# A mixture-of-experts loop on one core: two paired If/Else ladders per expert become three exclusive regions in a row, with a hint for the jump over the long one

## Chip, cores and metric

One core of a Trainium2 chip runs the whole program. The metric is device time in microseconds (us) per execution, the median of several runs. The engines are called as the profile calls them: PE (TensorE matmul), PEld (TensorE weight load; TensorE's own sequencer instructions stand under PEldq), DVE (VectorE), ACT (ScalarE), POOL (GpSimd), SP (SyncE, which here issues the weights' DMAs). A letter q behind an engine's name means its sequencer: branches, register loads, semaphores.

## What is computed

Two layers of a backbone over 1024 latent and 256 context tokens of width 1024. Each layer has a mixer (attention, pooling, convolution) and then a hierarchical mixture of 32 experts: the best of 4 groups, and in it the best 2 of 8 experts, so each token goes to 2 experts. The change is in the second part alone:

```python
def hier_moe(h, w_rg, b_rg, w_re, b_re, wg, wu, wd):
    lg = (h @ w_rg).astype(jnp.float32) + b_rg
    gsel = jnp.argmax(lg, axis=-1)
    ...
    top_v, top_i = lax.top_k(le_sel, TOP_K_IN_GROUP)
    ...
```

For every expert the tokens routed to it are multiplied by its gate and up matrices (1024 x 512 each), silu(gate) * up goes through its down matrix (512 x 1024), and the result is weighted and added up per token. One expert's three matrices are 6.29 MB in fp32. How many tokens an expert gets is known only at run time.

## The kernel before

**Tokens and paths.** Tokens of an expert are taken in chunks of 128. A register `n` per expert holds the number of started half chunks of 64 tokens (`load_n`, L2229). With `n` = 1 (37 of the 64 experts in the two layers with these inputs) the expert runs `half` (L2085): 32 matmuls in plain fp32 that put up to 64 tokens through gate and up. With `n` = 2 (17 experts) it runs `full` (L2109): 48 matmuls on split fp32r operands, three to a product, where ACT makes the high part and DVE the low part of every weight slice (`ws`, `self.split`, L167 and L168). With `n` above 2 (10 experts) there is a second chunk and more, with further Ifs inside (L2268, L2272, L2303, L2309).

**The loop over the experts** (L2256) is unrolled 32 times per layer, and the code of all paths of all experts lies in one long program. Per expert: the register load of a later `n`, a gather of the tokens of expert e+2 on POOL, then **the first ladder** (L2264: `n` below 2, else L2267: `n` above 2, else `full`), whose arms are gate and up alone; then for all arms alike `act` (Silu on ACT and a product on DVE, L2138), the transposes of the next expert's tokens (`xt_pe`, L2053) and of the hidden values (`ht`, L2144), then **the second ladder** (L2298, L2301) around `down` (L2154), then `prep` of the next expert if that has `n` above 1 (L2321: five splits each on ACT and DVE, `prep`, L2080), `evac` (L2162) and two scatters on POOL (`scatter`, L2168). Every engine takes every branch for itself: it loads `n` into its own register and runs its own copy of the Ifs.

**Weights** come through a ring of 14 buffers of 1 MB, six per expert (four for gate and up, two for down). `e_loads` (L2012) lets SP issue the loads for as many units as its limit says, each behind the release of the buffer; it is called once behind the first ladder and once at the expert's end. `over` (L2247) gathers an expert's second chunk, under an If.

Of the kernel before, what the change touches and what calls it, by code (L numbers as in the profile page):

```python
# [30 lines left out]
ALPHA = (2 * DEPTH) ** 0.25  # L31
EPS = 1e-6
OOB = 1 << 24

NU, NU0 = 14, 10

# [105 lines left out]
class Kernel:  # L142
# [1885 lines left out]
    def moe(self):  # L2028
        tc, nc, l = self.tc, self.nc, self.l
        nt = self.nt  # L2030
        T = nt * 128
        with ExitStack() as ctx:
# [3 lines left out]
            xg = [sp.tile([128, D], F32, name=f"xg{i}") for i in range(5)]  # L2036
# [11 lines left out]
            def gather(buf, idx):  # L2048
                nc.gpsimd.indirect_dma_start(out=buf, out_offset=None, in_=self.h_d[0:T, :],
                                             in_offset=bass.IndirectOffsetOnAxis(ap=idx, axis=0),  # L2050
                                             bounds_check=T - 1, oob_is_err=False)
# [11 lines left out]
            def xt_copy(tps, n):  # L2063
                nc.scalar.activation(XT[n % 2][:, 0:4, :], tps[0], AF.Copy)
                nc.vector.tensor_copy(XT[n % 2][:, 4:8, :], tps[1])
# [12 lines left out]
            def prep(e):  # L2078

                for k in range(AHEAD):  # L2080
                    ws(e, k)
                    if k < 2:
                        xs(e, 0, k)

            def half(ps, e):  # L2085


                x = XT[e % 2]
                for k in range(KD):
                    w = self.unit(e, k // 2)[:, k % 2]  # L2090
                    for o in range(2):
                        nc.tensor.matmul(ps[0][64 * o:64 * o + 64, :], x[:, k, 0:64], w[:, :, o * 256:(o + 1) * 256],  # L2092
                                         start=(k == 0), stop=(k == KD - 1))
# [15 lines left out]
            def full(ps, e, x=None):  # L2109

                for k in range(KD - 2):
                    if k + AHEAD < KD:
                        ws(e, k + AHEAD)
                    prod(ps, 0, k)
                for o in range(2):
                    for k in range(KD - 2, KD):
                        prod(ps, 0, k, NS, (o,))
                    if x is not None and o == 0:
                        xt(x, e)

            def double(ps, p2, e, m):

                prod(ps, 0, 0)
                xt(xg[2 + e % 3], e)
                for k in range(1, AHEAD):
                    prod(ps, 0, k)
                if m > 4:
                    gather(xg[2 + e % 3], self.idx_g[:, 2, e:e + 1])
                xs(e, 1, 0)
                xs(e, 1, 1)  # L2130
                for k in range(KD):
                    prod(p2, 1, k, NS - 1)
                    if k + NS - 1 < KD:
                        ws(e, k + NS - 1, NS - 1)
                    if AHEAD <= k + NS - 2 < KD:
                        prod(ps, 0, k + NS - 2, NS - 1)

            def act(ps, o):  # L2138
                sg = SG[o]
                nc.scalar.activation(sg, ps[o][:, 0:256], AF.Silu)  # L2140
                nc.vector.tensor_tensor(sg, ps[o][:, 256:512], sg, op=OP.mult)  # L2141
                return sg
# [7 lines left out]
            def hidden(ps, g):  # L2150
                for o, s in enumerate((act(ps, 0), act(ps, 1))):
                    ht(ps, s, g, o)

            def down(g, e, hf, os=range(2)):  # L2154
                for k, o in [(k, o) for k in range(4) for o in os] if hf else [(k, o) for o in os for k in range(4)]:
                        c = slice(o * 512, o * 512 + 512)
                        z = k // 2 * 64
                        nc.tensor.matmul(py[o][64 * o:64 * o + 64, :] if hf else py[o],  # L2158
                                         g[:, k % 2, z:z + 64] if hf else g[:, k, :],
                                         self.unit(e, 4 + k // 2)[:, k % 2, c], start=(k == 0), stop=(k == 3))  # L2160

            def evac(y):  # L2162
                nc.scalar.activation(y[:, 0:512], py[0], AF.Copy)
                nc.vector.tensor_copy(y[:, 512:1024], py[1])  # L2164
# [16 lines left out]
            def places(e, j):  # L2181
                return [x[:, j, e:e + 1] for x in (self.idx_v, self.idx_w)]
# [58 lines left out]
                nc.gpsimd.memset(x, 0.0)  # L2241
            xt(xg[0], 0)
            self.e_loads(NU, nc.scalar)
            with tc.If(N[0] > 1):
                prep(0)

            def over(e):  # L2247
                with tc.If(N[e] > 2):
                    gather(xg[2 + e % 3], self.idx_g[:, 1, e:e + 1])
            load_n(1)  # L2250
            load_n(2)
            over(0)
            over(1)
            over(2)
            self.route_rows(sp)
            for e in range(NE):  # L2256
                n = N.pop(e)
                nxt = e + 1 if e + 1 < NE else None
                if e + 3 < NE:
                    load_n(e + 3)  # L2260
                if e + 2 < NE:
                    gather(xg[e % 2], self.idx_g[:, 0, e + 2:e + 3])
                ps, p2, y, y2, g, g2 = GU[e % 2], GU[1 - e % 2], Y[e % 2], Y[1 - e % 2], G[e % 2], G[1 - e % 2]
                with tc.If(n < 2) as c:  # L2264
                    half(ps, e)
                with c.Else():
                    with tc.If(n > 2) as c2:  # L2267
                        with tc.If(n < 4) as c3:  # L2268
                            full(ps, e, xg[2 + e % 3])
                            half(p2, e)  # L2270
                        with c3.Else():
                            with tc.If(n > 4) as c4:  # L2272
                                double(ps, p2, e, 5)
                                hidden(p2, g2)
                                down(g2, e, False)
                                evac(y2)
                                scatter(y2, places(e, 1))
                                more(e, n, 2, p2, g2)
                            with c4.Else():
                                double(ps, p2, e, 4)  # L2280
                    with c2.Else():
                        full(ps, e)
                self.e_loads(e * 6 + 4 + NU)
                pl = sp.tile([128, 2], I32, name="pl", bufs=4)
                for o, z in enumerate(places(e, 0)):
                    nc.vector.tensor_copy(pl[:, o:o + 1], z)
                if e + 3 < NE:
                    over(e + 3)
                s0, s1 = act(ps, 0), act(ps, 1)
                if nxt:  # L2290
                    x = xt_pe(xg[nxt % 2], (0,))
                ht(ps, s0, g, 0)
                if nxt:
                    x += xt_pe(xg[nxt % 2], (1,))
                ht(ps, s1, g, 1)
                if nxt:
                    xt_copy(x, nxt)
                with tc.If(n < 2) as c:  # L2298
                    down(g, e, True)
                with c.Else():  # L2300
                    with tc.If(n > 2) as c2:  # L2301
                        down(g, e, False, (0,))
                        with tc.If(n < 5) as c3:  # L2303
                            s0, s1 = act(p2, 0), act(p2, 1)
                            ht(p2, s0, g2, 0)
                            ht(p2, s1, g2, 1)
                            down(g, e, False, (1,))
                            evac(y2)
                            with tc.If(n < 4) as c4:  # L2309
                                down(g2, e, True)  # L2310
                            with c4.Else():
                                down(g2, e, False)
                            scatter(y2, places(e, 0))
                            for o, z in enumerate(places(e, 1)):
                                nc.vector.tensor_copy(pl[:, o:o + 1], z)
                        with c3.Else():
                            down(g, e, False, (1,))
                    with c2.Else():
                        down(g, e, False)
                if nxt:  # L2320
                    with tc.If(N[nxt] > 1):  # L2321
                        prep(nxt)
                evac(y)
                self.e_loads(e * 6 + 6 + NU)
                scatter(y, [pl[:, o:o + 1] for o in range(2)])
                if e >= NE - 3:
                    self.marks.append(nc.gpsimd.memset(self.spacer, 0.0))
                if e == 2:
                    self.route_gates()
# [147 lines left out]
```

## Time and profile before

| what | value |
|---|---|
| median of 3 runs | 3215.24 us (3214.84 to 3216.71) |
| the profiled execution | 3213.33 us, its span 3211.5 us, granted TensorE clock 0.918 |
| PE busy | 2635.0 us, 82% of the span |
| DVE, ACT, POOL busy | 1493.3, 1188.0, 1070.6 us |
| expert stage of the first layer | from about 845 us to 1650 us |
| expert stage of the second layer | from about 2374 us to 3148 us |

The span runs from the first to the last instruction; the profiled time is 1.8 us more. TensorE is the busiest engine, but its share is an average over stages of different kinds; what concerns the change is how TensorE's idle time is spread over the two expert stages.

### The profile page before, as it was taken

The numbers are of one execution on the slowest core, as the hardware profiler recorded it, in microseconds if no ns is written. First come the engines' busy times: TensorE is split into PE (matmuls) and PEld (weight loads), VectorE is DVE, ScalarE is ACT, GpSimd is POOL, SyncE is SP. The second block draws the span as 40 slices with busy tenths as digits, with TensorE's granted clock in tenths as the row PEclk, the third lists the DMA queues.
The fourth block names the chain that finished last, engine by engine and source line by source line (L and its number), as shares of the span: only waits on it lengthen the run. The fifth ranks groups of instructions, "written<-read, shape, count | busy, mean of one in ns | idle before, by whom it ended". The sixth has DMA issues, their size and how long they took to land. (4 is left out here: it accounts for less than half of the span.)

```text
span 3211.5 us, 41598 instructions
## 1 busy us (share of the span) xinstructions
PE 2635.0 (82%) x13118; PEld 1663.1 (52%) x13118; DVE 1493.3 (46%) x2851; ACT 1188.0 (37%) x2260; POOL 1070.6 (33%) x919
## 2 busy tenths in 40 slices
PE   6988899998488769879757989999957788798783
PEld 4766565576254435455227766666732344554331
DVE  3355556487543323334149555556851332333215
ACT  3223666632143323333135337665211322333212
POOL 1023999223311121211136349941331111111114
PEclk8998999999799889999878999999978899899997
DMA  7542000042778685757976530002279876645995
GB/s 270 215 142 74 1 1 1 1 158 85 277 297 335 231 310 184 278 188 264 360 295 193 183 136 1 1 1 96 88 260 380 312 288 248 233 158 203 340 361 230
DMA packets 280605, 616.63 MB, mean 192 GB/s; under 512 B 63376, under 2 KB 77072, under 8 KB 271504
## 3 DMA queue, kind: packets, MB, share of 16 engines
q1 hardware_dynamic: 251696, 562.24, 47.9%
q0 software_dynamic: 24544, 37.91, 3.4%
q10 hardware_dynamic: 3712, 8.88, 0.7%
q8 instruction: 275, 4.51, 0.6%
q14 instruction: 378, 3.10, 0.3%
HBM read 577.09 MB, written 73.81 MB: 203 GB/s over the span
## 5 line engine op out<-in xcount | busy, mean ns | idle before, releaser
L1327 DVE TENSOR_REDUCE mx<-S 128x1 f32<-128x1024 f32 (+1 forms) x272 | 215.3, 798 | 208.9 <-PE S L1322 208.5
L172 PE MATMUL gu<-wh,xh 128*128 128x512 f32 x432 | 188.8, 437 | 119.2 <-issue 100.5
L2158 PE MATMUL mpy<-er,g 128*128 128x512 f32 (+1 forms) x672 | 242.8, 630 | 9.9 <-issue 7.3
L2172 POOL DMA_INDIRECT y_d<-my,pl x128 | 140.8, 1100 | 321.5 <-ACTq L2264 108.8
L1339 ACT ACTIVATE P<-S,nb 128x256 f32<-128x256 f32 (+1 forms) x272 | 208.6, 773 | 33.7 <-DVE nb L1331 32.6
L1353 ACT ACTIVATE PT<-pt 128x512 f32<-128x512 f32 (+1 forms) x321 | 169.3, 532 | 135.5 <-PE pt L1344 126.9
L2141 DVE TENSOR_TENSOR sg<-gu,sg 128x256 f32<-128x256 f32 x152 | 57.6, 420 | 342.5 <-ACT sg L2140 337.5
L2171 POOL MEMSET spacer<- 128x1 f32 x152 | 17.6, 116 | 595.7 <-DMA y_d<-my,pl 330.0
L1344 PE MATMUL pt<-ident,P 128*128 128x128 f32 x1312 | 206.7, 282 | 10.1 <-ACT P L1339 10.0
L1388 PE MATMUL po<-PT,V 128*64 128x256 f32 x1312 | 212.5, 403 | 0.1
L2059 PE MATMUL mtp<-ident,xg 128*128 128x128 f32 x600 | 101.1, 300 | 133.7 <-issue 83.3
L178 POOL TENSOR_TENSOR rs_out<-ln_ve,mhalf 128x1 f32<-128x1 f32 x64 | 58.8, 919 | 444.4 <-DVE ln_ve L197 287.8
L2140 ACT ACTIVATE sg<-gu 128x256 f32<-128x256 f32 x152 | 50.3, 383 | 411.3 <-PE gu L2092 285.3
L173 PE MATMUL gu<-wl,xh 128*128 128x512 f32 x432 | 183.0, 424 | 9.0 <-DVE wl L168 9.0
L1344 PEld LDWEIGHTS pt<-ident,P 128*128 128x128 f32 x1312 | 145.3, 141 | 83.4 <-ACT P L1339 41.5
L174 PE MATMUL gu<-wh,xl 128*128 128x512 f32 x432 | 181.4, 420 | 4.3 <-issue 4.3
L168 DVE TENSOR_TENSOR wl<-er,wh 128x1024 fp32r<-128x1024 f32 x102 | 124.3, 1223 | 108.7 <-ACT wh L167 105.1
L172 PEld LDWEIGHTS gu<-wh,xh 128*128 128x128 f32 x432 | 88.9, 206 | 164.9 <-issue 140.2
L2164 DVE COPY my<-mpy 128x512 f32<-128x512 f32 x75 | 51.7, 690 | 260.0 <-PE mpy L2158 252.1
L1321 PE MATMUL S<-KH,Q 128*128 128x512 f32 (+1 forms) x400 | 168.8, 423 | 1.5 <-ACT P L1339 1.5
L2059 PEld LDWEIGHTS mtp<-ident,xg 128*128 128x128 f32 x600 | 77.8, 155 | 173.8 <-issue 125.2
L2092 PE MATMUL gu<-er,xT 128*64 128x512 f32 x720 | 161.4, 594 | 3.2 <-DVEq L2264 2.3
(381 smaller groups left out, 6410.1 us busy)
## 6 DMA issues: line engine op xcount, KB each, us to landing
er<-in_w_e_down SPq DMA_DIRECT2D x66, 1024.0 KB
er<-in_w_e_gate SPq DMA_DIRECT2D x130, 512.0 KB
er<-in_w_e_up SPq DMA_DIRECT2D x130, 512.0 KB
raw<-in_w_mod SPq DMA_DIRECT2D x40, 1024.0 KB
es<-in_w_e_gate SPq DMA_DIRECT2D x64, 512.0 KB
es<-in_w_e_up SPq DMA_DIRECT2D x64, 512.0 KB
es<-in_w_e_down SPq DMA_DIRECT2D x32, 1024.0 KB
raw<-in_w_e_gate SPq DMA_DIRECT2D x40, 512.0 KB
```

Of the source, the lines that this page charges most:

```text
L172: t.matmul(ps, lh, rh, start=start, stop=False)
L173: t.matmul(ps, lh, rl, start=False, stop=False)
L174: t.matmul(ps, ll, rh, start=False, stop=stop)
L1321: tens.matmul(x[:, c:c + w], q, self.KH[:, g, o:o + w], start=True, stop=False)
L1327: v.tensor_reduce(S[st, "mx"][:, ci:ci + 1], S[st, ci][:, 0:cs[ci][1]], axis=AX.X, op=OP.max)
L1339: act.activation(P[st][:, c:c + w], S[st, ci][:, :w], AF.Exp, bias=S[st, "nb"], accum_out=SU[pi][:, i, h, ci:ci + 1])
L1344: tens.transpose(tp[:, j, :], P[st][:, (g_ * 4 + j) * 128:(g_ * 4 + j + 1) * 128], self.ident)
L1353: act.activation(d, TP[st, g_][:, :m, :], AF.Copy)
L1388: tens.matmul(PO[key][o * 64:o * 64 + 64, :], self.V[:, k0(pi) + j, hp // 2, :], PT[pi, 2 * hp + o][:, j, :], start=(j == 0), stop=(j == n ...
L2059: nc.tensor.transpose(tp[:, j, :], x[:, k * 128:(k + 1) * 128], self.ident)
L2092: nc.tensor.matmul(ps[0][64 * o:64 * o + 64, :], x[:, k, 0:64], w[:, :, o * 256:(o + 1) * 256], start=(k == 0), stop=(k == KD - 1))
L2158: nc.tensor.matmul(py[o][64 * o:64 * o + 64, :] if hf else py[o], g[:, k % 2, z:z + 64] if hf else g[:, k, :], self.unit(e, 4 + k // 2)[:, ...
```

## The change

Per expert, the two ladders become three regions in a row that exclude each other: `n` above 2 first (label, and marked so that its body follows its branch directly), then `n` below 2, then `n` equal to 2. Each holds the expert's whole work (gate and up, activation, transposes, down). `small` does one activation and one `ht` where the common code did two. `prep` of the next expert and the gather of `over` lose their Ifs and run always. The loads of an expert's six units are asked for in one call at its end. Right behind the `n` above 2 region stands a hint, on all five engines, that the branch of the next expert's `n` above 2 region is likely taken (taken means jumping over the region).

```diff
@@ -31,6 +31,7 @@
 ALPHA = (2 * DEPTH) ** 0.25
 EPS = 1e-6
 OOB = 1 << 24
+HINTED = [mybir.EngineType.PE, mybir.EngineType.Activation, mybir.EngineType.DVE, mybir.EngineType.Pool, mybir.EngineType.SP]
 
 NU, NU0 = 14, 10
 
@@ -2241,18 +2242,83 @@
                 nc.gpsimd.memset(x, 0.0)
             xt(xg[0], 0)
             self.e_loads(NU, nc.scalar)
-            with tc.If(N[0] > 1):
-                prep(0)
+            prep(0)
+            tc.mark_branch_hint_location(f"more{l}_0", "LikelyTaken", HINTED)
 
             def over(e):
-                with tc.If(N[e] > 2):
-                    gather(xg[2 + e % 3], self.idx_g[:, 1, e:e + 1])
+
+                gather(xg[2 + e % 3], self.idx_g[:, 1, e:e + 1])
             load_n(1)
             load_n(2)
             over(0)
             over(1)
             over(2)
             self.route_rows(sp)
+
+            def tokens(nxt, hs=range(2)):
+                return xt_pe(xg[nxt % 2], hs) if nxt else []
+
+            def small(e, nxt):
+
+                ps, g = GU[e % 2], G[e % 2]
+                half(ps, e)
+                s0 = act(ps, 0)
+                x = tokens(nxt)
+                ht(ps, s0, g, 0)
+                if nxt:
+                    xt_copy(x, nxt)
+                down(g, e, True)
+
+            def middle(ps, g, nxt):
+                s0, s1 = act(ps, 0), act(ps, 1)
+                x = tokens(nxt, (0,))
+                ht(ps, s0, g, 0)
+                x += tokens(nxt, (1,))
+                ht(ps, s1, g, 1)
+                if nxt:
+                    xt_copy(x, nxt)
+
+            def one_chunk(e, nxt):
+
+                ps, g = GU[e % 2], G[e % 2]
+                full(ps, e)
+                middle(ps, g, nxt)
+                down(g, e, False)
+
+            def chunks(e, n, nxt, pl):
+
+                ps, p2, y2, g, g2 = GU[e % 2], GU[1 - e % 2], Y[1 - e % 2], G[e % 2], G[1 - e % 2]
...
+
             for e in range(NE):
                 n = N.pop(e)
                 nxt = e + 1 if e + 1 < NE else None
@@ -2260,69 +2326,24 @@
                     load_n(e + 3)
                 if e + 2 < NE:
                     gather(xg[e % 2], self.idx_g[:, 0, e + 2:e + 3])
-                ps, p2, y, y2, g, g2 = GU[e % 2], GU[1 - e % 2], Y[e % 2], Y[1 - e % 2], G[e % 2], G[1 - e % 2]
-                with tc.If(n < 2) as c:
-                    half(ps, e)
-                with c.Else():
-                    with tc.If(n > 2) as c2:
...
-                    with c2.Else():
-                        full(ps, e)
-                self.e_loads(e * 6 + 4 + NU)
                 pl = sp.tile([128, 2], I32, name="pl", bufs=4)
                 for o, z in enumerate(places(e, 0)):
                     nc.vector.tensor_copy(pl[:, o:o + 1], z)
+                with tc.If(n > 2, label=f"more{l}_{e}", preferred_fallthrough_block=True):
+                    chunks(e, n, nxt, pl)
+                if nxt:
+                    tc.mark_branch_hint_location(f"more{l}_{nxt}", "LikelyTaken", HINTED)
+                with tc.If(n < 2):
+                    small(e, nxt)
+                with tc.If(n == 2):
+                    one_chunk(e, nxt)
+                self.e_loads(e * 6 + 6 + NU)
+                if nxt:
+                    prep(nxt)
+                evac(Y[e % 2])
                 if e + 3 < NE:
                     over(e + 3)
-                s0, s1 = act(ps, 0), act(ps, 1)
-                if nxt:
-                    x = xt_pe(xg[nxt % 2], (0,))
-                ht(ps, s0, g, 0)
-                if nxt:
-                    x += xt_pe(xg[nxt % 2], (1,))
-                ht(ps, s1, g, 1)
-                if nxt:
-                    xt_copy(x, nxt)
-                with tc.If(n < 2) as c:
-                    down(g, e, True)
-                with c.Else():
-                    with tc.If(n > 2) as c2:
-                        down(g, e, False, (0,))
...
-                    with c2.Else():
-                        down(g, e, False)
-                if nxt:
-                    with tc.If(N[nxt] > 1):
-                        prep(nxt)
-                evac(y)
-                self.e_loads(e * 6 + 6 + NU)
-                scatter(y, [pl[:, o:o + 1] for o in range(2)])
+                scatter(Y[e % 2], [pl[:, o:o + 1] for o in range(2)])
                 if e >= NE - 3:
                     self.marks.append(nc.gpsimd.memset(self.spacer, 0.0))
                 if e == 2:
```

What is left out at the new `chunks` is the two-and-more-chunk code of both ladders, put behind one another without change of its order.

On TensorE, at an expert's end and the next one's beginning, before (L2158 is down, L2092 half's gate and up of the next expert; what stands in brackets are semaphores that the instruction waits for):

```order
L2158 MATMUL mpy_7379<-raw,g_7392 128x512 [waits DMAHW6_49]
L2158 MATMUL mpy_7379<-raw,g_7392 128x512
L2301 UNCONDITIONAL_BRANCH
L2321 COMPARE_AND_BRANCH
L2321 UNCONDITIONAL_BRANCH x2
L2230 TENSOR_LOAD nch
L2264 COMPARE_AND_BRANCH
L2092 MATMUL gu_7376<-er_7085,xT_7398 64x512 [waits DMAHW5_49,DVE_49,DMAHW6_49,Activation_49]
```

The same place now (L2159 is down of the `n` = 2 arm, L2332 the branch over the long region):

```order
L2159 MATMUL mpy_7379<-es_7380,g_7393 128x512 x2
L2159 MATMUL mpy_7379<-es_7381,g_7393 128x512 x2
L2338 UNCONDITIONAL_BRANCH
L2338 UNCONDITIONAL_BRANCH [waits PE_49]
L2231 TENSOR_LOAD nch
L2332 COMPARE_AND_BRANCH
L2291 COMPARE_AND_BRANCH
```

The second branch of L2338 is the arm of an expert that skips the region. It now waits for PE's own semaphore, which counts PE's finished matmuls; before, the branches at this place waited for nothing. The order of the paths on TensorE now, behind the long region:

```order
L2332 UNCONDITIONAL_BRANCH [waits PE_49,PE_sequencer_49]
L2485 BRANCH_PREFETCH_HINT
L2336 COMPARE_AND_BRANCH
L2093 MATMUL gu_7374<-es_7382,xT_7397 64x512 [waits DMAHW0_49,DVE_49,DMAHW7_49,PE_49,Activation_49]
L2093 MATMUL gu_7374<-es_7382,xT_7397 64x512 x3
```

The long region lies between L2332's branch and the hint; the hint's branch is that of the next expert, which comes behind `half` and `full` of this one.

On ACT, before, the activation of a layer's fourth expert (L2140 Silu, L2148 and L2064 copies; its table load is the last one in the layer's experts):

```order
L2140 ACT_TABLE_LOAD
L2140 ACTIVATE sg_7394<-gu_7376 128x256
L2140 ACTIVATE sg_7395<-gu_7377 128x256
L2148 ACTIVATE g_7393<-gu_7376 128x256
L2148 ACTIVATE g_7393<-gu_7377 128x256
L2064 ACTIVATE xT_7397<-mtp 128x512
L2298 COMPARE_AND_BRANCH
```

Now, the same expert's `n` below 2 arm and the beginning of its `n` equal to 2 arm (L168 split):

```order
L2336 COMPARE_AND_BRANCH
L2141 ACT_TABLE_LOAD
L2141 ACTIVATE sg_7394<-gu_7376 128x256
L2149 ACTIVATE g_7393<-gu_7376 128x256
L2065 ACTIVATE xT_7397<-mtp 128x512
L2336 UNCONDITIONAL_BRANCH x2
L2338 COMPARE_AND_BRANCH
L168 ACT_TABLE_LOAD
L168 ACTIVATE wh_7390<-er_7088 128x1024
```

And the join behind the arms, where `prep` of the next expert begins:

```order
L2065 ACTIVATE xT_7397<-mtp 128x512
L2338 UNCONDITIONAL_BRANCH x2
L168 ACT_TABLE_LOAD
L168 ACTIVATE wh_7384<-es_7380 128x1024
L168 ACTIVATE xh<-xT_7397 128x512
```

The program has 13 table loads on ACT before and 357 now: from the fourth expert of a layer on, one ahead of Silu in every arm, one ahead of `full`'s splits, one ahead of `prep`'s.

## Rows read from the trace of the kernel before

**Rows 1.** The page: busy time of the engines.
```profile
PE 2635.0 (82%) x13118; PEld 1663.1 (52%) x13118; DVE 1493.3 (46%) x2851; ACT 1188.0 (37%) x2260; POOL 1070.6 (33%) x919
```

**Rows 2.** Stretches: length; PE, PEld, DVE, ACT, POOL busy; clock, DMA share, GB/s.
```profile
865.00:1512.00 647.00, 529.70 (x2078) 315.45 (x2075) 244.04 (x354) 226.71 (x349) 114.13 (x146) 0.93 0.71 262
1512.00:1645.00 133.00, 107.61 (x471) 41.21 (x469) 18.14 (x47) 19.10 (x47) 24.08 (x40) 0.91 0.94 346
2388.00:2536.00 148.00, 111.36 (x481) 43.59 (x480) 24.38 (x77) 25.24 (x55) 24.92 (x38) 0.87 1.01 374
2536.00:3022.00 486.00, 404.78 (x1543) 241.76 (x1544) 170.34 (x241) 157.33 (x246) 75.84 (x109) 0.94 0.64 237
3022.00:3148.00 126.00, 100.87 (x474) 41.43 (x472) 18.83 (x48) 21.08 (x52) 25.88 (x43) 0.97 0.96 348
```

**Rows 3.** The page's costliest groups: count | busy, mean ns | idle before, releaser.
```profile
L172 PE MATMUL gu<-wh,xh 128*128 128x512 f32 x432 | 188.8, 437 | 119.2 <-issue 100.5
...
L2059 PE MATMUL mtp<-ident,xg 128*128 128x128 f32 x600 | 101.1, 300 | 133.7 <-issue 83.3
```

**Rows 4.** Branches and register loads by line, whole span: ns minimum/median/maximum.
```profile
L2264 PEldq COMPARE_BRANCH  x101: 67/217/7411, 860.3 to 3130.9; - x101
L2264 DVEq COMPARE_BRANCH  x101: 43/50/69, 865.6 to 3128.6; - x101
L2267 PEldq COMPARE_BRANCH  x27: 68/6030/8056, 877.3 to 2992.8; - x27
L2298 PEldq COMPARE_BRANCH  x101: 68/211/5717, 872.2 to 3142.2; - x101
L2230 PEldq TENSOR_LOAD <-nch x64: 297/306/490, 844.9 to 3084.6; - x64
```

**Rows 5.** Timeline of PE, an n = 1 expert and the next, n = 2.
```profile
929.68 7.09 PE L2092 MATMUL gu<-er,xT 128*64 128x512 f32 x32
939.31 0.63 PE L2059 MATMUL mtp<-ident,xg 128*128 128x128 f32 x4 [2.54 <-DVE sg L2141]
940.74 1.94 PE L2158 MATMUL mpy<-er,g 128*64 128x512 f32 x8
...
952.61 0.77 PE L172 MATMUL gu<-wh,xh 128*128 128x512 f32 x1 [8.22 <-issue]
```

**Rows 6.** The three long branches of that stretch, one line each.
```profile
L2264 PEldq COMPARE_BRANCH  x1: 6277/6277/6277, 932.5 to 932.5; - x1
L2298 PEldq COMPARE_BRANCH  x1: 4108/4108/4108, 940.8 to 940.8; - x1
L2267 PEldq COMPARE_BRANCH  x1: 6475/6475/6475, 946.0 to 946.0; - x1
```

**Rows 7.** Timeline of PE, an n = 2 expert's down and the next, n = 2.
```profile
901.44 7.10 PE L2158 MATMUL mpy<-es,g 128*128 128x512 f32 x16
909.22 0.47 PE L172 MATMUL gu<-wh,xh 128*128 128x512 f32 x1 [0.68 <-issue]
```

**Rows 8.** Timeline of PE, an n = 1 expert that follows another's down.
```profile
2440.25 7.03 PE L2092 MATMUL gu<-er,xT 128*64 128x512 f32 x32
2449.85 0.63 PE L2059 MATMUL mtp<-ident,xg 128*128 128x128 f32 x4 [2.57 <-issue]
```

**Rows 9.** PE's waits from 2388 to 2536 us: total, times, longest.
```profile
PE mtp L2059 <- issue: 29.0, 8, 7.5
PE mpy L2158 <- DMA er<-in_w_e_gate: 2.3, 1, 2.3
```

**Rows 10.** ACT: a table load by line, and the timeline ahead of full.
```profile
L2140 ACT ACT_TABLE_LOAD  x2: 1283/1283/1283, 935.3 to 2445.8; - x2
...
942.20 1.06 ACT L167 ACTIVATE wh<-es 128x1024 fp32r<-128x1024 f32 x1 [0.48 <-DMA er<-in_w_e_gate]
```

**Rows 11.** The page's queue of TensorE's code: packets, MB, share; and POOL's gathers by line.
```profile
q8 instruction: 275, 4.51, 0.6%
L2049 POOL DMA_INDIRECT xg<-h_d,idx_g x75: 997/1047/2096, 853.6 to 3107.8; - x75
```

More of the change, by code (lines that the diff above doesn't have):

```diff
@@ L2255, in moe @@
             self.route_rows(sp)
+            def tokens(nxt, hs=range(2)):
[24 more added lines that the diff above has]
+                ps, p2, y2, g, g2 = GU[e % 2], GU[1 - e % 2], Y[1 - e % 2], G[e % 2], G[1 - e % 2]
+                with tc.If(n < 4) as c3:
+                    full(ps, e, xg[2 + e % 3])
+                    half(p2, e)
+                with c3.Else():
+                    with tc.If(n > 4) as c4:
+                        double(ps, p2, e, 5)
+                        hidden(p2, g2)
+                        down(g2, e, False)
+                        evac(y2)
+                        scatter(y2, places(e, 1))
+                        more(e, n, 2, p2, g2)
+                    with c4.Else():
+                        double(ps, p2, e, 4)
+                middle(ps, g, nxt)
+                down(g, e, False, (0,))
+                with tc.If(n < 5) as c3:
+                    s0, s1 = act(p2, 0), act(p2, 1)
+                    ht(p2, s0, g2, 0)
+                    ht(p2, s1, g2, 1)
+                    down(g, e, False, (1,))
+                    evac(y2)
+                    with tc.If(n < 4) as c4:
+                        down(g2, e, True)
+                    with c4.Else():
+                        down(g2, e, False)
+                    scatter(y2, places(e, 0))
+                    for o, z in enumerate(places(e, 1)):
+                        nc.vector.tensor_copy(pl[:, o:o + 1], z)
+                with c3.Else():
+                    down(g, e, False, (1,))
             for e in range(NE):
@@ L2262, in moe @@
                     gather(xg[e % 2], self.idx_g[:, 0, e + 2:e + 3])
-                ps, p2, y, y2, g, g2 = GU[e % 2], GU[1 - e % 2], Y[e % 2], Y[1 - e % 2], G[e % 2], G[1 - e % 2]
-                with tc.If(n < 2) as c:
-                    half(ps, e)
-                with c.Else():
-                    with tc.If(n > 2) as c2:
[L2268 to L2280, printed above, removed]
-                    with c2.Else():
-                        full(ps, e)
-                self.e_loads(e * 6 + 4 + NU)
                 pl = sp.tile([128, 2], I32, name="pl", bufs=4)
@@ L2300, in moe @@
-                with c.Else():
-                    with tc.If(n > 2) as c2:
-                        down(g, e, False, (0,))
[L2303 to L2317, printed above, removed]
-                    with c2.Else():
-                        down(g, e, False)
```

## The prediction, made before the changed kernel was run

> **What bounds the kernel now.** I read the page first, then the stretches, then the costliest groups, the branches by line, and the timeline at single experts. The page puts PE at 82% of the span and no other engine above 52% [rows 1]; so TensorE sets the time, and what a change can win is TensorE's idle time. The five stretches show where that lies in the expert stages: length less PE busy is 117.3, 25.4, 36.6, 81.2 and 25.1 us, 285.6 together [rows 2]. The groups say what ends it: in front of the first matmul of `full` 100.5 us, and in front of the transposes of the next expert's tokens 83.3 us are put down to "issue", to no engine and no DMA [rows 3]. Within 2388 to 2536 us, the stretch with the most DMA, PE waits 29.0 us for issue and 2.3 us for a weight [rows 9].
>
> The branches tell what "issue" is. On DVE a branch takes at most 69 ns. On TensorE's sequencer the ones of L2264 and L2298 take some 0.2 us in the median and up to 7.4 and 5.7, that of L2267 6.0 in the median [rows 4]. The short value is a branch whose target is at hand, the long one a jump over so much code that the target has to be fetched. One expert pair shows how it hurts. The sequencer runs ahead of the matmuls: at 932.5, inside `half` (929.68 to 936.77), it begins the jump over the long else arm, 6.28 us, and the transposes stand 2.54 us idle behind `half`. Down is issued, the next jump takes 4.11 us, and the third, to `full`, 6.48 us from 946.0: `full` begins at 952.61, 8.22 us after down [rows 5, 6]. From `full` to `full` the same jump is hidden behind a down of 7.10 us, and 0.68 us are left [rows 7]. So a jump costs what stands behind the cover that the queued matmuls give, from 0 to 6.3 us.
>
> I sorted the 62 passages from one expert to the next by their pair of n and read from the timeline what each loses against full pace (7.0 and 3.7 us for `half` and its down, 11.4 and 7.1 for `full`'s, 2.0 between). In us, on the mean: 1 to 1, 23 times 4.0; 1 to 2, 7 times 7.7; 2 to 1, 9 times 4.4; 2 to 2, 5 times 3.9; 1 to more, 5 times 7.8; more to 2, 5 times 4.5; more to 1, 3 times 2.1; 2 to more, 3 times 1.5; more to more, twice 0.4. That is 279 us, against 285.6 of idle in the stretches [rows 2].
>
> **Part by part.** *The ladders.* Each n = 1 or 2 expert had two or three long jumps; it now has one, over the long region, of some 1,430 TensorE instructions by the program's list. *The cover.* Here the change takes something away. An expert that skips a region now waits for PE's own semaphore, as the order of instructions shows, so the sequencer can't reach the next expert's register load and jump before down has run out. From the end of down come then the register load, 0.31 us, a branch of 0.22 [rows 4], their semaphores, and the first matmul's own start; I take 1.7 us for 1 to 1 if the jump's target is there. Before, that passage had no idle time between down and `half` [rows 8]; its loss lay behind `half`, 2.57 us, and that goes. Behind an n = 2 expert the jump is made while down runs, and 0.9 to 1.2 us of drain are left, whatever the hint does.
>
> *The hint.* No row shows one executed. Its two ends are 0.2 us for the jump (all fetched) and the 6.2 us of a jump that begins with nothing at hand [rows 4, 6]. The hint stands a whole expert ahead of its branch, and TensorE runs through one or more further pieces of code in between (TensorE's queue of code moved 4.51 MB in 275 packets, 16 KB each [rows 11]). I take the middle: the fetch is asked for, but only when the engine comes into the piece of code in which the hinted branch stands, so that about down's time (3.7 to 7.1 us) covers it. The passages then cost: 1 to 1, 3.8 (2.5 with all fetched, since some `half` runs into a piece not yet there; 8.4 with nothing); 1 to 2, 7.3 (6.0; 11.7); 2 to 1, 0.9; 2 to 2, 1.2; 1 to more, 8.4 (8.0; 8.0), since that path has its inner jumps as before, now uncovered; more to 2, 8.1 (5.6; 11.4); more to 1, 6.7 (2.5; 8.4); 2 to more, 3.0 (2.3; 2.3); more to more, 5.7 (4.7; 4.7). Sums, of the unrounded means: middle 277, all fetched 206, nothing 428. Against 279 that is -2, -73 and +148 us.
>
> [...]
>
> *ACT's tables.* One load is 1.283 us [rows 10]. An n = 1 expert now makes two, the others two or three: some 130 in all, 167 us of ACT. ACT is busy 37% [rows 1], and the load ahead of Silu runs while PE is still in `half`. It is exposed where `prep` feeds a `full` at once: the splits from 942.20, with 0.48 us idle before them [rows 10]; 12 passages, at most 15 us. I have it in the 7.3 and 8.1 above as a floor of 2.3 us from down to `full`. If all 130 were exposed it would be +167; PE's Silu wait begins only when `half` ends, 7.09 us after its start [rows 5], and that excludes it.
>
> *prep and the gathers, always.* For an n = 1 expert next, ACT gets five splits (at most 1.06 us each [rows 10]), and evac waits behind them. Nothing needs evac before the next down, 9.6 us after `half` begins [rows 8]; cost 0. Without that cover it would be up to 5.3 us each. 54 more gathers of 1.05 us lie on POOL [rows 11], which is busy 33% [rows 1]: 0. *One activation instead of two* at n = 1: 0.35 us each on PE, in the figures. *The loads in one call*: SP still waits buffer by buffer, 0.
>
> *Weights.* From 2388 to 2536 us eight n = 1 experts run with the DMA engines at 1.01 and 374 GB/s [rows 2]. The middle case would take 21 us out of that stretch; 6.29 MB per expert at 374 GB/s are 16.8 us, against some 14.4 for an expert at full speed (7.0 + 2.0 + 3.7 and 1.7 of drain). The ring's lead of 14 buffers, 2.3 experts, pays for part. I give back 10 of the 21 (between 0 and 21). The four passages into and at the end of the layers, not in the pairs, I put at 1 us each, +4.
>
> Sum, against the profiled execution: 3213.3 - 2 + 10 + 4 = 3225.3. The median of the runs is 1.9 us above that execution, so 3227.
>
> **The rivals.** *The hint works in full* (the target is fetched at once and kept). For it: it is set 10 us or more ahead, and one fetch is 6.2. Against: no row shows code kept that isn't next in line. -73, of which the weights give back 10 to 20: 3150 to 3165. This ends on the other side; it decides once a quarter of the 71 us between the two sums is won, since 18 us take the middle case's +12 below -6. *The hint does nothing*, so that a jump of 6.2 us stands open behind each drained n = 1 expert: +148, 3363; with half of what lies between it and the middle case, 3290. For it: each drain takes the 4 us of cover that the trace shows [rows 5, 6]; it decides if the 1 to 1 passage, 4.0 us before, comes out nearer to 8.4 than to 3.8. *The weights bound the runs of n = 1*: clock and jumps then don't matter there; on its own it makes the gain of the first rival 40 us, 3175.
>
> **How the numbers follow.** A difference under 0.2%, 6.4 us, can't be told from none. Middle case, 0.45, spread 3205 to 3255 by the weights' bounds and the floors: a sixth of it faster than 3208.8, a quarter the same, the rest slower. Hint in full, with or without the weights' bound, 0.32: faster. Hint without effect or nearly, 0.23: slower. Faster 0.32 + 0.07 = 0.39, same 0.12, slower 0.26 + 0.23 = 0.49. The range runs from 3152, which leaves out a few of the first rival, to 3320, which leaves out half of the second.
>
> **What would show it.** The branch over the long region (L2332): about 0.2 us everywhere is the first rival, 6 us behind n = 1 is the second, and a mixture, by where the branch stands in its piece of code, is mine. Between down and `half` some 1.7 us or more should stand where there was nothing, and the 2.5 us behind `half` should be gone. ACT should be about 170 us busier by table loads alone, POOL 60, with no PE wait on either above 2.3 us. I am wrong if L2332 is the same everywhere, or if PE's new waits name ACT, POOL or a DMA.

## The result, and the profile after

The change takes 3481.48 us in the median (3470.28 to 3486.68), against 3215.04 us before: a ratio of 1.083, 95% interval 1.080 to 1.087, slower by 266 us and above the range that was given. The profiled execution has a span of 3477.6 us.

The page, beside [rows 1] and [rows 3] of before:

```profile
PE 2679.8 (77%) x13044; PEld 1670.3 (48%) x13044; DVE 1646.7 (47%) x2999; ACT 1476.6 (42%) x2501; POOL 1174.8 (34%) x973
...
L173 PE MATMUL gu<-wh,xh 128*128 128x512 f32 x432 | 194.6, 450 | 196.7 <-DVEq L2336 103.5
...
L2093 PE MATMUL gu<-er,xT 128*64 128x512 f32 x720 | 199.9, 713 | 139.1 <-DVEq L2332 129.7
...
L168 ACT ACT_TABLE_LOAD x71 | 91.1, 1283 | 228.3 <-PEq L2338 139.3
```

And the row of `half` on the page of before:

```profile
L2092 PE MATMUL gu<-er,xT 128*64 128x512 f32 x720 | 161.4, 594 | 3.2 <-DVEq L2264 2.3
```

Ahead of `half` (L2093) and of `full` (L173) PE now waits for a sequencer instruction of DVE, where it waited for "issue" or hardly at all. The transposes (L2059, now L2060) wait 2.6 us for issue in place of 83.3. PE's longest waits over the whole span (engine, line, releaser: us in total, times, longest):

```profile
PE gu L2093 <- DVEq L2332: 253.9, 36, 13.6
PE gu L173 <- DVEq L2336: 103.5, 15, 9.8
PE gu L173 <- issue: 56.8, 6, 15.4
```

The same five stretches of the expert stages, cut at the same experts as [rows 2]:

```profile
865.00:1572.00 707.00, 547.36 (x2076) 326.09 (x2077) 281.36 (x403) 314.36 (x421) 146.97 (x164) 0.88 0.67 243
1572.00:1755.00 183.00, 118.87 (x470) 42.64 (x468) 51.62 (x79) 66.79 (x88) 36.76 (x45) 0.81 0.65 232
2514.00:2695.00 181.00, 115.09 (x464) 41.02 (x464) 47.92 (x78) 56.86 (x81) 37.73 (x44) 0.80 0.75 271
2695.00:3223.00 528.00, 407.25 (x1521) 243.97 (x1522) 193.63 (x262) 226.13 (x303) 102.20 (x122) 0.88 0.61 222
3223.00:3407.00 184.00, 118.91 (x470) 42.53 (x468) 52.32 (x80) 67.87 (x91) 36.75 (x45) 0.81 0.64 227
```

They are 1783 us long, before 1540: +243 of the span's +266. PE's idle time in them is 475.5 us in place of 285.6, +190, and its busy time 1307.5 in place of 1254.3, +53. The second part goes with the clock: in the three stretches of `n` = 1 experts 0.80 or 0.81 is granted, where it was 0.87 to 0.97 with less idle time between the matmuls, and a matmul of `half` takes 713 ns in place of 594. The other 23 us lie outside the stretches, 16 of them between the second and the third stretch, before the second layer's first `half`.

The branches on TensorE's sequencer, to be read beside [rows 4] (L2332 is the long region's, L2336 the one for `n` below 2):

```profile
L2332 PEldq COMPARE_BRANCH  x64: 86/447/7198, 859.3 to 3382.8; - x64
L2336 PEldq COMPARE_BRANCH  x101: 76/192/6438, 860.5 to 3402.4; - x101
```

So the jump over the long region is no longer slow: 0.45 us in the median. What is slow is seen in one passage from an `n` = 1 expert to the next, on PE, then ACT, then DVE:

```profile
1729.68 3.65 PE L2159 MATMUL mpy<-er,g 128*64 128x512 f32 x16 [0.47 <-ACT g L2149]
1741.47 1.97 PE L2093 MATMUL gu<-er,xT 128*64 128x512 f32 x4 [8.14 <-DVEq L2332]
```

```profile
1729.52 0.59 ACT L2065 ACTIVATE xT<-mtp 128x512 f32<-128x512 f32 x1
1733.50 1.28 ACT L168 ACT_TABLE_LOAD   x1 [3.39 <-PEq L2338]
1734.80 1.06 ACT L168 ACTIVATE wh<-er 128x1024 fp32r<-128x1024 f32 x1
...
1738.70 0.57 ACT L2164 ACTIVATE my<-mpy 128x512 f32<-128x512 f32 x1
1741.45 1.28 ACT L2141 ACT_TABLE_LOAD   x1 [2.18 <-DVEq L2332]
```

```profile
1735.89 1.23 DVE L169 TENSOR_TENSOR wl<-er,wh 128x1024 fp32r<-128x1024 f32 x1 [6.30 <-ACT wh L168]
...
1739.37 1.22 DVE L169 TENSOR_TENSOR wl<-er,wh 128x1024 fp32r<-128x1024 f32 x1
1740.50 0.69 DVE L2165 COPY my<-mpy 128x512 f32<-128x512 f32 x1
1741.11 0.14 DVE L2331 COPY pl<-idx_v 128x1 int32<-128x1 int32 x1
1741.16 0.15 DVE L2331 COPY pl<-idx_w 128x1 int32<-128x1 int32 x1
```

Down ends at 1733.33. Only then PE passes the skip arm of the `n` = 2 region (L2338), and only that releases ACT: a table load, the splits of `prep`, evac; DVE follows each split with its low part, then its half of evac and the two copies of `pl`. After these DVE passes the skip arm of the next expert's long region (L2332), and 0.2 us later `half` begins. Work that could lie beside `half` stands in one chain between down and `half`: 8.14 us. This passage is a typical one: 8.14 us is also the median of the 38 waits of `half` behind a down in this trace.

The theory, called *joins* below: three Ifs in a row are not known to exclude each other. What reads or overwrites a tile that an earlier region touches waits for that region's end on its engine, also where the region is skipped. `prep` overwrites the split weights that the `n` = 2 region reads, so ACT waits for PE's skip arm there (3.39 us above); `half` uses the PSUM and token tiles that the long region uses, so PE waits for DVE's skip arm there (8.14 us above), which stands behind `prep` and evac in DVE's order. Rivals: *fetch* (the loss is in jumps after all) and *tables* (the loss is the ACT table loads).

### The profile page after: what moved, and what is told of

The parts are those of the page before. It is cut to its first block, busy times and chain, and to the rows that moved or that the text cites. A ratio compares the mean times of both kernels' runs of the same rounds, so it can differ in the third digit from the quotient of the medians.

```text
span 3477.6 us, 41317 instructions
## 1 busy us (share of the span) xinstructions
PE 2679.8 (77%) x13044; PEld 1670.3 (48%) x13044; DVE 1646.7 (47%) x2999; ACT 1476.6 (42%) x2501; POOL 1174.8 (34%) x973
## 5 line engine op out<-in xcount | busy, mean ns | idle before, releaser
L2173 POOL DMA_INDIRECT y_d<-my,pl x128 | 200.1, 1563 | 627.3 <-ACTq L2332 427.3
L173 PE MATMUL gu<-wh,xh 128*128 128x512 f32 x432 | 194.6, 450 | 196.7 <-DVEq L2336 103.5
L169 DVE TENSOR_TENSOR wl<-er,wh 128x1024 fp32r<-128x1024 f32 x163 | 198.9, 1223 | 273.6 <-ACT wh L168 255.5
L2093 PE MATMUL gu<-er,xT 128*64 128x512 f32 x720 | 199.9, 713 | 139.1 <-DVEq L2332 129.7
L2050 POOL DMA_INDIRECT xg<-h_d,idx_g x129 | 133.8, 1038 | 467.0 <-PE gu L175 125.6
L2142 DVE TENSOR_TENSOR sg<-gu,sg 128x256 f32<-128x256 f32 x115 | 47.8, 424 | 488.8 <-ACT sg L2141 488.7
L2159 PE MATMUL mpy<-er,g 128*128 128x512 f32 (+1 forms) x672 | 230.4, 598 | 10.1 <-ACT g L2149 9.5
L2141 ACT ACTIVATE sg<-gu 128x256 f32<-128x256 f32 x115 | 43.1, 387 | 416.0 <-PE gu L2093 333.8
L173 PEld LDWEIGHTS gu<-wh,xh 128*128 128x128 f32 x432 | 93.0, 215 | 240.3 <-issue 218.4
L168 ACT ACTIVATE wh<-er 128x1024 fp32r<-128x1024 f32 x163 | 171.6, 1054 | 82.5 <-PE gu L175 63.3
L2093 PEld LDWEIGHTS gu<-er,xT 128*64 128x64 f32 x720 | 65.2, 163 | 269.2 <-issue 267.2
L169 DVE TENSOR_TENSOR wl<-es,wh 128x1024 fp32r<-128x1024 f32 x87 | 106.4, 1223 | 140.5 <-ACT wh L168 133.6
```

Source lines behind the costliest of these rows:

```text
L168: self.nc.scalar.activation(h, src, AF.Copy)
L169: (eng or self.nc.vector).tensor_tensor(l, src, f32(h), op=OP.subtract)
L173: t.matmul(ps, lh, rh, start=start, stop=False)
L2173: s = nc.gpsimd.indirect_dma_start(out=self.y_d[0:2 * T, :].rearrange("t (h d) -> (t h) d", h=2), out_offset=bass.IndirectOffsetOnAxis(ap= ...
```

## Experiments

**1. No hints.** Both hint lines are taken out.

```diff
-            tc.mark_branch_hint_location(f"more{l}_0", "LikelyTaken", HINTED)
...
-                if nxt:
-                    tc.mark_branch_hint_location(f"more{l}_{nxt}", "LikelyTaken", HINTED)
```

> The change without its hints, the three regions as they are. Theory (joins): each half starts when DVE has passed the skip arm of the long region, about 8.1 us after down; a jump of 6.2 us that starts when PE has drained ends before that. So L2332's branch goes from 0.45 us in the median to about 6, if it was the hint that shortened it, and the time stays within 40 us of 3481. Rival (fetch): the loss of the change is in jumps that the hint does not help; then L2332 stays as it is and the time too, within 5 us. Rival (tables): no difference from the theory here.

Measured: 3477.46 us, ratio to before 1.083 (1.080 to 1.086), 4 us below the change, which is no difference beside the spread of the runs. The branch over the long region, here L2331:

```profile
L2331 PEldq COMPARE_BRANCH  x64: 77/5942/7561, 863.2 to 3380.2; - x64
```

The hint does work: 0.45 against 5.94 us. In the change it gains nothing: the slow jump ends before DVE's chain does, and PE's longest wait is still the one of `half` for DVE at this line (225.7 us in 32 waits, 253.9 in 36 with hints). The time alone would also fit fetch. What speaks against it is the branch, which fetch would have left as it was, and what PE waits for; fetch falls.

**2. prep under its If again**, as before (and the same at `prep(0)`).

```diff
                 if nxt:
-                    prep(nxt)
+                    with tc.If(N[nxt] > 1):
+                        prep(nxt)
```

> The change with prep of the next expert under its If again (n above 1), as before. Theory (joins): behind an n = 1 or 2 expert with an n = 1 expert next, DVE no longer has splits and ACT no longer its table load between PE's drain and the skip arm of the long region; the gap in front of half falls from 8.1 us to 2 to 4 us, and with some 35 such passages the time falls by 140 to 200 us, to 3280 to 3340. Rival (fetch): no more than 10 us. Rival (tables): one load of 1.28 us per such passage less, about 45 us, to 3435.

Measured: 3301.82 us, ratio 1.028 (1.025 to 1.031), 180 us below the change. PE's timeline from an `n` = 1 expert's down to the next `half`:

```profile
2458.96 3.65 PE L2159 MATMUL mpy<-er,g 128*64 128x512 f32 x16 [0.47 <-ACT g L2149]
2464.76 5.37 PE L2093 MATMUL gu<-er,xT 128*64 128x512 f32 x24 [2.15 <-PEq L2333]
```

The gap is 2.15 us in place of 8.14 (medians 2.24 and 8.14), and PE's own sequencer ends it. `full` is as before this edit: it still waits 103.1 us for DVE's skip arm. The table loads became more, where the expectation had them fall: 157 run in the experts (ahead of Silu, `evac` and the splits) against 132 in the change. So this gain is not theirs.

**3. One Silu behind the gates' Exp.** A skip of all three regions could leave Exp's table in place, as far as the build can know; one Silu ahead, on a tile of one element, rules that out, and 11 loads run in the whole program, as before, in place of 141.

```diff
                 if e == 2:
                     self.route_gates()
+                    nc.scalar.activation(one_silu, one_silu, AF.Silu)
```

> The change with one Silu of one element behind the gates' Exp, which leaves the Silu table in place, so that the program has 13 table loads on ACT again in place of 357; nothing else differs. Theory (joins): one load of 1.28 us goes out of the chain drain, prep, evac, skip arm: gaps of 8.1 us become 6.9, about 50 passages, minus 50 to 80 us, to 3400 to 3430. Rival (tables): the loads are the main loss, minus 200 or more, to below 3280. Rival (fetch): under 10 us.

Measured: 3407.93 us, ratio 1.061 (1.058 to 1.065), 74 us below the change. PE's timeline at such a passage:

```profile
2498.56 1.98 PE L2095 MATMUL gu<-er,xT 128*64 128x512 f32 x4 [6.86 <-DVEq L2334]
```

The gap is shorter by 8.14 - 6.86 = 1.28 us (6.86 is the median too), one load of ACT to the hundredth, on an engine that PE does not wait for directly. The loads are part of the chain and not the main loss.

**4. Nested.** The same paths, hint and `prep` always, but as If and Else.

```diff
-                with tc.If(n > 2, label=f"more{l}_{e}", preferred_fallthrough_block=True):
+                with tc.If(n > 2, label=f"more{l}_{e}", preferred_fallthrough_block=True) as c:
                     chunks(e, n, nxt, pl)
-                if nxt:
-                    tc.mark_branch_hint_location(f"more{l}_{nxt}", "LikelyTaken", HINTED)
-                with tc.If(n < 2):
-                    small(e, nxt)
-                with tc.If(n == 2):
-                    one_chunk(e, nxt)
+                with c.Else():
+                    if nxt:
+                        tc.mark_branch_hint_location(f"more{l}_{nxt}", "LikelyTaken", HINTED)
+                    with tc.If(n < 2) as c2:
+                        small(e, nxt)
+                    with c2.Else():
+                        one_chunk(e, nxt)
```

> The same three paths, the same order in the program and the same hint, but nested as If and Else (n above 2, else n below 2, else), so that the arms are known to exclude each other. Prep and the gathers still run always. Theory (joins): half and full no longer wait for a skip arm on DVE and PE no longer for its own drain; PE's waits on DVEq at L2332 and L2336 (357 us in the change) go nearly to nothing, and the time falls by 250 us or more, to 3230 or below. The table loads go too (17 in the program). Rival (fetch): still above 3400. Rival (tables): to about 3310, with the DVEq waits still there.

Measured: 3170.24 us, ratio 0.987 (0.983 to 0.990): 311 us below the change, 42 below before. PE's longest waits, and the stretch of eight `n` = 1 experts:

```profile
PE gu L173 <- issue: 117.8, 13, 13.4
PE tp L837 <- ACT xn L818: 44.6, 8, 30.5
...
PE gu L2093 <- issue: 18.4, 5, 10.8
```

```profile
2370.00:2499.00 129.00, 101.46 (x458) 38.48 (x454) 60.38 (x111) 52.96 (x82) 37.01 (x47) 0.95 1.00 372
```

The DVEq waits of `half` and `full` are gone; this stretch took 148 us before, at a clock of 0.87, and 181 in the change, at 0.80. One more thing differs: the hint stands in the Else, so that an expert behind one of `n` above 2 is not hinted. Run 10 puts that back, and the time is the same. So this run shows that it is the missing exclusion of the arms that makes the change a loss: with it, the rest of the change together gains 42 us. It removes the joins, the drain and the table loads together, so it does not price each. The medians of `half`'s wait behind a down do in part: 8.14 us in the change, 6.86 without the loads (run 3), 2.24 without `prep` (run 2), 1.41 nested.

**5. Nested, prep under its If.** The diffs of runs 2 and 4 together.

> The nested version with prep of the next expert under its If again. Theory (joins): with the joins gone nothing of PE waits for prep unless a full follows, so taking 37 preps away gives little: within 20 us of the nested version's 3170. Rival (prep's work itself is what cost 180 us in the change): 100 us or more below it.

Measured: 3196.63 us, ratio 0.995 (0.993 to 0.997), 26 us *above* the nested version. The rival falls: the same edit is worth -180 us with the joins and +26 without. That is outside the 20 us that were expected: the If itself costs something. PE's waits for issue ahead of `full` and of `half` are 136.2 and 32.1 us here, 117.8 and 18.4 in the nested version.

**6. Nested, no hints.** The diffs of runs 1 and 4 together.

> The nested version without hints. In it the branch over the long region still takes 4.3 us in the median, so the hint helps little there. Theory (the hint's fetch starts when the piece of code with the hinted branch is entered, and behind n = 1 that is the jump just before it): the branch goes to 6 us in the median, from 0.35 to 6 behind n = 2 where down covers most of it; time plus 10 to 50 us. Rival (hint worth nothing here): within 5 us. Rival (hint prefetches from where it stands): plus 100 us or more.

Measured: 3269.14 us, ratio 1.018 (1.013 to 1.023), 99 us above the nested version, twice what was expected and near the rival's value. The branch with the hint (L2332, nested) and without it (L2331, this run):

```profile
L2332 PEldq COMPARE_BRANCH  x64: 73/4264/7277, 859.5 to 3076.1; - x64
```

```profile
L2331 PEldq COMPARE_BRANCH  x64: 67/6608/7644, 860.7 to 3172.7; - x64
```

By its single records it goes behind `n` = 1 from 4.70 to 6.78 us on the mean, 30 times, and behind `n` = 2 from 1.38 to 6.63, 14 times: 136 us, of which down hides some. My size failed in part because I took 6 us for an unhinted jump; here it is nearer 7, 6.61 in the median. The packets of TensorE's code in the two traces show why: between the jump out of the `n` = 1 arm and the end of the branch one packet arrives in all 30 cases with the hint, and two arrive in 29 of 30 without it. In both the last one ends 1.4 us (median) before the branch does. So without the hint one more packet comes first; what code it holds was not shown.

**7. Before, with prep always** (and the same at `prep(0)`), nothing else.

```diff
                 if nxt:
-                    with tc.If(N[nxt] > 1):
-                        prep(nxt)
+                    prep(nxt)
```

> The kernel before with one edit of the change alone: prep of the next expert always. Theory (joins): five splits more on ACT and DVE per n = 1 expert lie beside half, no PE wait, 0 to 20 us above 3212. Rival (prep's work itself costs): 100 us or more above.

Measured: 3198.85 us, ratio 0.996 (0.993 to 0.998): 14 us below before, where 0 to 20 above was expected. Prep's work costs nothing there, and the If costs a little; PE's wait for issue ahead of `full` falls from 100.5 to 77.1 us [rows 3]. Run 5 agrees, where putting the If back costs 26 us. Whether that is the branch or where the code now falls in its pieces was not tried.

**8. Long region last**, with the one Silu of run 3; the three regions still stand in a row.

```diff
+                with tc.If(n < 2):
+                    small(e, nxt)
+                with tc.If(n == 2):
+                    one_chunk(e, nxt)
                 with tc.If(n > 2, label=f"more{l}_{e}", preferred_fallthrough_block=True):
                     chunks(e, n, nxt, pl)
                 if nxt:
                     tc.mark_branch_hint_location(f"more{l}_{nxt}", "LikelyTaken", HINTED)
-                with tc.If(n < 2):
-                    small(e, nxt)
-                with tc.If(n == 2):
-                    one_chunk(e, nxt)
```

> Three regions in a row as in the change, but the long one last (n below 2, n equal to 2, n above 2), with the one Silu behind the gates' Exp, so it is to be compared with that run (3408). Theory (joins): half's joins are now those of the preceding expert, which DVE passes before prep and evac, so half waits only for PE's drain, register load and branch, about 2 us in place of 6.9 behind down; 100 to 170 us less, 3240 to 3310. Rival (any regions in a row cost this): within 30 us of 3408.

Measured: 3344.04 us, ratio 1.040 (1.035 to 1.045), 64 us below run 3, where the theory had 100 to 170: between theory and rival. `full` is why, as PE's longest waits over the span show:

```profile
PE gu L173 <- issue: 110.2, 6, 24.2
PE gu L173 <- DVEq L2334: 72.8, 10, 10.1
PE gu L2095 <- ACT wh L168: 50.6, 15, 8.8
```

No wait of `half` for DVE's skip arm is left among PE's longest, as the theory has it, but it still waits 50.6 us for ACT's splits, and `full` now waits for the skip arm of the `n` below 2 region (L2334). The six waits of 110.2 us stand ahead of the chunk code, which is now reached over the two short regions: in the longest, 24.2 us, three branches of 4.8, 7.4 and 7.6 us follow one another. I had reckoned with `half` alone.

**9. Nested, arms swapped.** Against run 4:

```diff
-                    with tc.If(n < 2) as c2:
-                        small(e, nxt)
-                    with c2.Else():
-                        one_chunk(e, nxt)
+                    with tc.If(n > 1) as c2:
+                        one_chunk(e, nxt)
+                    with c2.Else():
+                        small(e, nxt)
```

> The nested version (3170) with its two short arms in the other order, n equal to 2 first, n below 2 second; the hint as it was. Theory (the hint's fetch starts when TensorE's sequencer comes into the piece of code that holds the hinted branch): an n = 1 expert now runs straight into the join instead of jumping into it, so the fetch starts earlier, while half is being issued, and the branch over the long region behind n = 1 falls from 4 to 6 us to under 2 in most cases; behind n = 2 it rises from 0.35 us to some 3 to 5, under the cover of down. Against that an n = 1 expert pays for the jump over the n equal to 2 arm where that crosses a piece not yet there. Time between 3110 and 3180. Rival (the hint's fetch starts where the hint stands or only at the branch): the branch behind n = 1 stays at 4 to 6 us.

Measured: 3186.63 us, ratio 0.992 (0.989 to 0.995), 16 us above the nested version and just above the expected band. By the single records the branch behind `n` = 1 falls from 4.70 to 2.47 us, 14 of 30 under 1 us, not "most"; behind `n` = 2 it rises from 1.38 to 3.28. The direction is the theory's; the new jump over the `n` = 2 arm, up to 6.36 us, eats it: PE's waits for issue fall from 117.8 to 70.8 us ahead of `full` and rise from 18.4 to 94.4 ahead of `half`.

**10 and 11. The hint in more places**: also at the start of the long arm (10), or once, ahead of this expert's own long region (11). Against run 4:

```diff
                 with tc.If(n > 2, label=f"more{l}_{e}", preferred_fallthrough_block=True) as c:
+                    if nxt:
+                        tc.mark_branch_hint_location(f"more{l}_{nxt}", "LikelyTaken", HINTED)
                     chunks(e, n, nxt, pl)
```

```diff
+                if nxt:
+                    tc.mark_branch_hint_location(f"more{l}_{nxt}", "LikelyTaken", HINTED)
                 with tc.If(n > 2, label=f"more{l}_{e}", preferred_fallthrough_block=True) as c:
                     chunks(e, n, nxt, pl)
                 with c.Else():
-                    if nxt:
-                        tc.mark_branch_hint_location(f"more{l}_{nxt}", "LikelyTaken", HINTED)
```

> The nested version (3170) with the hint for the next expert's branch also at the start of the long arm, so that an expert behind one of n above 2 is hinted too; in the nested version those eight branches take 7.0 us, each uncovered. Theory (a hint acts when the piece of code with its branch is entered, however long ago it was set): those eight fall by 1 to 6 us, as they did in the change, and the time by 10 to 40 us, to 3130 to 3160. Rival (a hint is forgotten over the many jumps of the long arm): within 8 us of 3170.

> The nested version with the hint for the next expert's branch set in front of this expert's own long region instead of inside the other arm, for all experts. Theory as before, if several hints are kept at a time: the same as with the hint in both arms, 3130 to 3160. Rival (a new hint replaces the one before, which then is lost where its fetch had not begun): branches behind n = 2 go from 0.37 us back toward 6, the time to 3190 or above.

Measured: 3169.48 us, ratio 0.986 (0.984 to 0.988), and 3157.23 us, ratio 0.982 (0.980 to 0.984). In both the eight branches behind an expert of `n` above 2 fall from 7.01 to 5.2 and 5.1 us, by 14 to 15 us in sum, and those behind `n` = 2 stay at 1.4, so here a hint survived the long arm and a second hint beside it. Run 10's time does not show the gain, run 11's does (13 us below the nested version); the branches of the two hardly differ, and the lowest run of 10 (3158.68) is as fast as the slowest of 11 (3158.70), so what parts their times stays open. Run 11 is the fastest version found, 56 us below before.

## Why the prediction was wrong

**The bound** was read rightly: TensorE's idle time, and in it the jumps. The ladders' jumps did go: L2059's waits for issue with them, 83.3 us before and 2.6 now.

**The hint** came out between its two ends, as the middle case had it, but the change alone does not show that: its branch, with a drain ahead of it, takes 0.45 us in the median, and 41 of the 52 jumps over the long region behind another expert take less than 1 us, which the first rival would have too. The nested version parts them: 0.37 us in the median behind `n` = 2, with down as cover, and 5.14 behind `n` = 1 without it. There the packet of code that the branch waits for starts 10.5 to 19.4 us behind the hint, but 3.5 us (median) behind the jump that leads to the branch; without hints the first packet starts 3.2 us behind that jump. So there that packet began behind the jump, and not at the hint. That what sets it off is the sequencer's entry into the branch's piece of code was the middle case's assumption; no run shows it. That the long branches wait for code, the trace of before shows: a packet of TensorE's code ends inside 97 of the 98 that took over 1 us, in the median 1.4 us before the branch does, and inside 1 of the 389 others. In the change all 11 branches of L2332 above 1 us have one inside and none of the 53 others. So the hint takes the wait for code away, if not everywhere: 0.45 against 5.94 us in the median (run 1).

**The step that failed** is "The cover", with "prep and the gathers, always" behind it. I took 1.7 us for 1 to 1, from PE's own semaphore, and put prep and evac at 0 because "Nothing needs evac before the next down". Something did: not evac's result but DVE's place in its queue. The order of instructions has `half`'s first matmul wait for DVE and ACT, before as well as now, and I gave that wait no price. Now it was one for the skip arm behind evac, and 1 to 1 cost 8.14 us. (The 9.6 us that I gave evac as cover end at the transposes [rows 8], not at down; in [rows 5] down begins 1.4 us later. Nothing hangs on it.) Likewise I had `prep` run beside down as before; it waits for PE's skip arm, so it starts when down has ended. What I named as the mark of an error, PE's new waits on ACT, POOL or a DMA, should have had DVE as well.

**ACT's tables**: some 130 loads were forecast, and 71 + 59 = 130 ran ahead of the splits and of Silu. Their place was wrong: not 12 passages and at most 15 us, but every passage in which PE waits for the chain, 74 us in run 3.

**The clock** was left out: PE's busy time in the stretches rose by 53 us, at a granted clock of 0.80 to 0.88 where it was 0.87 to 0.97, with 475.5 us of idle time in place of 285.6. In the nested version it is 0.91 to 0.95.

**The weights** bound nothing in the change: the share of the DMA engines in the stretch that had 1.01 fell to 0.75. In the nested version it is at 1.00, and there that bound is near.

The second rival's 3363 (3367 with the 4 us at the layers' ends, which that sum leaves out) lay nearer, and its sign came true too: the 1 to 1 passage, at 8.14 us, is nearer to 8.4 than to 3.8. But that is luck: run 1 rules its reason out, since without any hint the time is the same. The length of the gap could not tell a jump from a join; what ends the gap could.

## What to carry to other kernels

Regions that exclude each other should be written as arms of one If: here that is 3170.24 us against 3481.48 (run 4). In a row, each was here a join for the engines that share a tile with it, also where it is skipped, and `half`'s wait on DVE's semaphore was a wait for everything ahead of the skip arm in DVE's queue: 8.14 us in the median behind a down, 1.41 nested. So for each wait of a first instruction ask which point of the other engine's program it names, not which data it needs; work that was free beside the bound (here `prep` for every expert, which cost nothing in the kernel before, run 7, and 180 us in the change, run 2) can become the path.

## What the hardware showed that was not expected

A hinted jump takes 0.45 us where the unhinted one takes 5.94 (run 1), and the profile's count of 16 KB code packets falls with it: 275 before, 279 without hints, 228 with them. So the hinted jumps come with fewer packets and not with more, nearly one less for each. The change jumps over the long region 54 times, all hinted, and moves 51 fewer than run 1. Of the nested version's 54 jumps 46 are hinted in run 4, and it moves 231 packets in place of run 6's 276, 45 fewer; in run 10 all are, and it moves 224, 52 fewer. The page's row of the change:

```profile
q8 instruction: 228, 3.74, 0.5%
```

And run 1:

```profile
q8 instruction: 279, 4.57, 0.6%
```

In run 11 a hint set a whole expert ahead still worked, past other jumps and past another hint: the branches behind `n` = 2 stay at 1.4 us on the mean, where they take 6.6 without hints (run 6).
